# Hybrid encoder layer on one core: six pairs of projection units by seven half products, rotary rows turned in groups

## The chip, the cores and the metric

The kernel runs on one core of one Trainium2 chip. The metric is the device time of one execution in microseconds (us); what counts is the median of several runs, and a change is worth telling from about 0.2% on.

## What is computed

One encoder layer on 512 tokens of 1024 channels, in float32. Two token mixers work on the same input: a windowed grouped-query attention (A: 16 query heads, 4 key and value heads, 64 wide, window 128, a sink logit for each head) and a mixture of three dilated window attentions (B: 3 groups of 4 heads). The first 16 channels of each head of q and k are rotated by position. Both mixers' outputs go through projections, are weighted by sigmoid gates, projected, normalised, and followed by a SwiGLU layer:

```python
proj = h @ w_in[l]
qa, ka, va, qb, kb, vb = jnp.split(proj, SPLITS, axis=-1)
qa = rope_partial(qa.reshape(b, s, A_Q_HEADS, HEAD_DIM), pos)
...                                   # ka, qb, kb are rotated likewise
o_a = windowed_gqa_sink(qa, ka, va, a_sink[l]).astype(h.dtype)
o_b = dilated_mixture(qb, kb, vb).astype(h.dtype)
gates = jax.nn.sigmoid(h @ w_gate[l] + b_gate[l])
g_a, g_b = jnp.split(gates, N_BRANCH, axis=-1)
mixed = g_a * (o_a @ w_br_a[l]) + g_b * (o_b @ w_br_b[l])
h = layer_norm(DN_ALPHA * h + mixed @ w_out[l], ln1_g[l], ln1_b[l])
f = (jax.nn.silu(h @ w_ff_gate[l]) * (h @ w_ff_up[l])) @ w_ff_down[l]
h = layer_norm(DN_ALPHA * h + f, ln2_g[l], ln2_b[l])
```

`rope_partial` of a pair (t1, t2) of 8 channels each is (t1·cos − t2·sin, t1·sin + t2·cos).

## The kernel before

**Products.** Every float32 operand is split into a high part (rounded, written by ScalarE or VectorE) and a low part (value minus high part, a subtraction on VectorE), both in the format fp32r that TensorE takes. A product is three matmuls: high·high, high·low, low·high. The work on the projections goes in units: 128 output channels for all 512 tokens. `unit` loads a unit's weights in two halves of 256 KB (`half_unit`: one DMA, one `split`), and `feat_x` runs 8 × 3 matmuls of 512 columns over the token tiles `xh`, `xl` (`feat_k`, L496 to L498) into one PSUM bank.

**The stages.** First x and the first weights come in pieces, and k0, q0 and v0 are multiplied as they land. Then the attention stage: units of q, k, gates (g), values (VA, V0, V12) and the attentions themselves (A0 to A3, B0 to B3: four blocks of queries each). One block of `unit_a` is scores, mask and row maximum (VectorE, L798), exp (ScalarE), reciprocal and normalisation (VectorE, L805, L739), turning of the probabilities by TensorE (L749), their split (the low part on VectorE, L754) and the product with the values, "p·v" (L815, L816). About 330 us from the start the branch projections, the output projection and the feed-forward stage follow.

**Rotary.** `rotate` takes a unit's result in PSUM, multiplies it by a table of cosines (L517), exchanges the two groups of 8 channels by a shuffle (L519), multiplies by a table of sines (L521) and adds (L523): four VectorE operations of 128×512 for each q or k unit, though only 16 rows of each 64 turn (the tables hold 1 and 0 elsewhere).

**Seven half products.** The feed-forward stage computes its units in pairs by the Strassen-Winograd scheme: the 2×2 blocks are (unit, half of the input channels) for the weights and (half of the input channels, half of the tokens) for the tokens. Weight forms A11, A12, A22 and S1 to S4 (sums), token forms B11, B21, B22 and T1 to T4; each of seven products has 12 matmuls of 256 columns (`Quad`, L1422 to L1424). S1 and S3 come from a load and a second, accumulating load by GpSimd's queue (`load_sum`, L368); S2 and S4 from an addition on VectorE.

**What sets the order.** `Program` is a list scheduler that runs while the kernel is built. Each operation has engines it may run on, a cost, what it reads and writes, and a priority: its place in the work of TensorE plus an offset (weights −130, results −100, normalisation −150; lower goes first). With a model of the engines it writes out one fixed sequence for each engine; on the chip each engine goes through its sequence in order, and waits where an input isn't there. `ORDER` gives the succession of the units. Buffers come from pools with limits: `ws` (weights as loaded, 6), `whl` (their high and low parts, 12), `att`, `gen`, and PSUM banks (3 for `dense`).

Of the kernel before, what the change touches and what calls it, by code (L numbers as in the profile page):

```python
# [9 lines left out]
F32 = mybir.dt.float32  # L10
# [49 lines left out]
BANKS = dict(dense=3, s=2, tb=2, o=1, d=8)  # L60
UNITS = 2
SPIN = 4

# [4 lines left out]
X_PACE = {1: None}  # L68
N_WS, N_WHL, N_ATT = 6, 12, 16

# [47 lines left out]
class Program:  # L118
# [67 lines left out]
    def run(self):  # L186
# [26 lines left out]
        while n_left:  # L213
# [11 lines left out]
            while progress:  # L225
                progress = False
                for e in engines:
# [88 lines left out]
def hybrid_layer(ctx: ExitStack, tc: tile.TileContext, wpack, xT, xtok, sink, bgate,  # L316
# [8 lines left out]
    pr = Program({"slot": N_SLOT, "bank": 8, **BANKS,  # L325
                  "ws": N_WS, "whl": N_WHL, "att": N_ATT, "gen": N_SLOT - 2 - N_ATT - N_WS - N_WHL,
                  "unit": UNITS, "st": 4, "x4": 4, "wf": N_WF})
# [46 lines left out]
    def cp_alts(n, ps=False, cut=0.0):  # L374
        return [(ACT, act(n, ps) + cut), (DVE, dve(n, not ps) + cut)]
# [79 lines left out]
    got = {}  # L455
    for j in range(KD):
        st, ap = slot(F32, "xs"), FIRST["x"][j]

        for c0, c1 in ((0, S // 2), (S // 2, S)) if j == 0 else ((0, S),):
# [49 lines left out]

    EV, NORM = -100.0, -150.0  # L510


    SHUF = list(range(8, 16)) + list(range(0, 8)) + list(range(16, 32))

    def rotate(ps):
        R, Sh = slot(), slot()
        op([(DVE, dve(S))], lambda e: nc.vector.tensor_tensor(halves(R.t), back(ps.t), halves(cosT.t), op=ALU.mult),  # L517
           reads=[ps, cosT], writes=[R], prio=EV)
        op([(DVE, dve(S, extra=0.03))], lambda e: nc.vector.stream_shuffle(halves(Sh.t), back(ps.t), SHUF), reads=[ps], writes=[Sh],  # L519
           prio=EV)  # L520
# [131 lines left out]
    def turned_values(u, nt, turn_by=0, done=None):  # L652
# [3 lines left out]
        for i in range(2):  # L656
# [15 lines left out]

            op(cp_alts(S, True, 0.3 if turn_by else 0.1)[:2 if turn_by else 1], evac, reads=[ps], writes=[t], prio=EV)
            src.append(t)
# [325 lines left out]
    away = {}  # L1000

    def gate(f, put=False):
        ps = bank("dense")
# [34 lines left out]
    load(mB, maskb, prio=0)  # L1038
    env = {"gate": 0, "qs": {}, "ks": {}}

    def step(w):
        if w == "VA":
            env["va"] = turned_values(U_VA, 4, 0, psv)
# [14 lines left out]
        elif w[0] in "QK":  # L1058
            pair, g = int(w[1]), int(w[2])
            u = U_QKB + 6 * pair + 2 * g + (w[0] == "K")  # L1060
# [201 lines left out]

    def copy_by_act(dst, src, n, ps, reads, writes, prio=NORM):
        op([(ACT, act(n, ps))], lambda e: copy(ACT, dst(), src()), reads=reads, writes=writes, prio=prio)

    h1h4, h1l4 = [x4(), x4()], [x4(), x4()]
# [39 lines left out]

    LO, HI = slice(0, HP), slice(HP, S)
    su, uf = {}, {}
    silus = []

    def tt(dst, x, y, o, reads, writes, w=HP, prio=EV):
        op([(DVE, dve(w))], lambda e: nc.vector.tensor_tensor(dst(), x(), y(), op=o), reads=reads, writes=writes,  # L1312
           prio=prio)

    def parts(h, l, src, reads, n, prio, whole=True):

        copy_by_act(h[0], src, n, False, reads, [h[1], l[2]], prio)
        tt(l[0], src, lambda: f32(h[0]()), ALU.subtract, [*reads, h[1]], [l[1]], n, prio)

    def hl(st, prio):  # L1320
        h, l = slot(F32R, "whl"), slot(F32R, "whl")
        parts((lambda: h.t, h), (lambda: l.t, l, (l, "room")), lambda: st.t, [st], S, prio)
        return h, l

# [450 lines left out]
```

## Time and profile before

| | |
|---|---|
| median of 3 runs | 737.42 us (737.29 to 737.45) |
| the profiled execution | 737.0 us, span 735.2 us |
| granted TensorE clock | 0.999 |
| TensorE / VectorE / ScalarE busy | 99% / 89% / 61% of the span |
| matmuls | 4479, starting with the warm-up |
| DMA | 120.17 MB, 163 GB/s over the span |

A row of the profile names the line of the kernel, the engine, the operation and the tiles (out<-in by the program's names: `ps` is a PSUM bank, `sl` a slot in SBUF, `x` a part of the tokens). Helpers that record many operations have one line for all of them, as L357 (copy on ScalarE) and L1312 (VectorE operation on two tensors). The time that one matmul takes overlaps with the next; the price of a matmul in a stream is the distance between two starts.

### The profile page before, as it was taken

To read this page: it belongs to the slowest core of one execution; us is meant where nothing else is said; L and a number is where in the kernel's file an instruction comes from. 1 tells how busy PE (TensorE), PEld (TensorE's weight loads), DVE (VectorE), ACT (ScalarE), POOL (GpSimd) and SP (SyncE) were. 2 spreads that over 40 slices of the span, in tenths; PEclk is the share of its full clock that TensorE was granted. 3 is DMA by queue.
4 is the path that set the end of the run, shared out by engine and by line. 5 is a ranking of instruction groups with operands and counts; after the bars stand their busy time and mean duration, and the time that the engine had idled before them with its cause. 6 is when DMAs were issued, how large, how long until landed. Compare 5 with 4: busy or idle time off the path is not lost.

```text
span 735.2 us, 13431 instructions
## 1 busy us (share of the span) xinstructions
PE 725.2 (99%) x4479; PEld 663.0 (90%) x4479; DVE 653.7 (89%) x1428; ACT 447.4 (61%) x1012; POOL 109.5 (15%) x273
## 2 busy tenths in 40 slices
PE   9999999999999999999999999999999999999995
PEld 6888888888888889888888999999999999999985
DVE  5879998898898999897686999799999999899977
ACT  5647687757665657774352567656666556666721
POOL 0000110000003323500010002111102111202100
PEclk9999999999999999999999999999999999999999
DMA  8824523437234765455583389776888978978402
GB/s 270 289 58 144 163 82 87 129 94 204 76 93 138 201 176 163 137 170 174 165 205 88 86 250 233 178 179 154 203 254 195 221 196 237 243 196 180 112 29 86
DMA packets 69252, 120.17 MB, mean 163 GB/s; under 512 B 8576, under 2 KB 12800, under 8 KB 69184
## 3 DMA queue, kind: packets, MB, share of 16 engines
q1 hardware_dynamic: 59040, 101.10, 44.7%
q0 software_dynamic: 9872, 18.09, 15.2%
q8 instruction: 35, 0.57, 0.3%
q14 instruction: 33, 0.27, 0.1%
q10 hardware_dynamic: 272, 0.13, 0.1%
HBM read 103.04 MB, written 2.10 MB: 143 GB/s over the span
## 4 chain that ended last, share of the span: by engine, by line
PE 94%; DMA 2%; DVE 2%; SPq 1%; ACT 1%; issue 0%; DVEq 0%; ACTq 0%
PE ps L497 12%; PE ps L496 12%; PE ps L498 12%; PE ps L1422 9%; PE ps L1424 9%; PE ps L1423 9%; PE ps L1633 4%; PE ps L1635 4%; PE ps L1634 4%; PE ps L749 3%; PE ps L1192 3%; PE ps L1193 3%; PE ps L1194 3%; PE ps L647 1%; PE ps L646 1%; PE ps L815 1%
## 5 line engine op out<-in xcount | busy, mean ns | idle before, releaser
L357 ACT ACTIVATE sl<-sl 128x512 fp32r<-128x512 f32 (+3 forms) x383 | 210.6, 582 | 62.0 <-DVE sl L1312 17.3
L1312 DVE TENSOR_TENSOR sl<-sl,sl 128x512 fp32r<-128x512 f32 (+3 forms) x294 | 167.1, 609 | 6.2 <-ACT sl L357 3.4
L357 ACT ACTIVATE sl<-ps 128x256 f32<-128x256 f32 (+5 forms) x205 | 85.8, 441 | 99.7 <-PE ps L1424 60.1
L496 PE MATMUL ps<-x,sl 128*128 128x512 f32 (+1 forms) x369 | 142.4, 386 | 0.3 <-ACT x L357 0.3
L498 PE MATMUL ps<-x,sl 128*128 128x512 f32 (+1 forms) x369 | 139.8, 379 | 0.0
L497 PE MATMUL ps<-x,sl 128*128 128x512 f32 (+1 forms) x337 | 127.9, 379 | 0.2 <-DVE x L469 0.2
L1422 PE MATMUL ps<-sl,sl 128*128 128x256 f32 x352 | 96.9, 275 | 0.6 <-ACT sl L357 0.6
L1423 PE MATMUL ps<-sl,sl 128*128 128x256 f32 x352 | 96.8, 275 | 0.0
L1424 PE MATMUL ps<-sl,sl 128*128 128x256 f32 x352 | 96.8, 275 | 0.0
L383 DVE TENSOR_TENSOR sl<-sl,sl 128x512 fp32r<-128x512 f32 x130 | 87.2, 685 | 5.1 <-ACT sl L357 4.5
L498 PEld LDWEIGHTS ps<-x,sl 128*128 128x128 f32 x369 | 69.9, 189 | 9.9 <-DVE sl L406 0.2
L496 PEld LDWEIGHTS ps<-x,sl 128*128 128x128 f32 x369 | 70.2, 190 | 8.7 <-ACT x L357 0.5
L371 POOL DMA_DIRECT2D sl<-wpack x44 | 38.5, 883 | 260.3 <-DMA sl<-wpack 72.7
L1422 PE MATMUL ps<-x,sl 128*128 128x256 f32 x264 | 72.6, 275 | 0.0
L1423 PE MATMUL ps<-x,sl 128*128 128x256 f32 x264 | 72.6, 275 | 0.0
L1424 PE MATMUL ps<-x,sl 128*128 128x256 f32 x264 | 72.6, 275 | 0.0
L497 PEld LDWEIGHTS ps<-x,sl 128*128 128x128 f32 x337 | 64.0, 190 | 7.5 <-DVE x L469 0.5
L1422 PEld LDWEIGHTS ps<-sl,sl 128*128 128x128 f32 x352 | 67.6, 192 | 0.8 <-ACT sl L357 0.7
L1423 PEld LDWEIGHTS ps<-sl,sl 128*128 128x128 f32 x352 | 67.6, 192 | 0.1
L1424 PEld LDWEIGHTS ps<-sl,sl 128*128 128x128 f32 x352 | 67.6, 192 | 0.0
L1422 PEld LDWEIGHTS ps<-x,sl 128*128 128x128 f32 x264 | 50.6, 192 | 0.4
L1423 PEld LDWEIGHTS ps<-x,sl 128*128 128x128 f32 x264 | 50.6, 192 | 0.4
(151 smaller groups left out, 1547.1 us busy)
## 6 DMA issues: line engine op xcount, KB each, us to landing
sl<-wpack SPq DMA_DIRECT2D x243, 256.0 KB, 3.7
sl<-sl SPq DMA_DIRECT2D x108, 128.0 KB, 2.3
wf<-wpack SPq DMA_DIRECT2D x51, 256.0 KB, 5.0
sl<-wpack POOLq DMA_DIRECT2D x44, 256.0 KB, 5.9
wf<-wpack POOLq DMA_DIRECT2D x24, 256.0 KB, 6.3
sl<-xtok SPq DMA_DIRECT2D x8, 256.0 KB, 3.3
out<-sl SPq DMA_DIRECT2D x7, 256.0 KB, 2.0
sl<-xT SPq DMA_DIRECT2D x6, 256.0 KB, 5.6
```

The lines of the kernel that those rows point to most:

```text
L357: nc.scalar.activation(dst, src, AF.Copy)
L371: op([(POOL, 1.0)], lambda e: nc.gpsimd.dma_start(b.t, src2, accum_op=ALU.add), reads=[b], writes=[b], prio=prio, moves=1.65)
L383: op([(DVE, dve(S))], lambda e: nc.vector.tensor_tensor(l.t, src.t, f32(h.t), op=ALU.subtract), reads=[src, h], writes=[l], prio=prio, abs ...
L496: mm(o, a, x0, start=(k == 0 and begins), stop=False, skip_group_check=split)
L497: mm(o, a, x1, start=False, stop=False, skip_group_check=split)
L498: mm(o, b, x0, start=False, stop=(k == nk - 1), skip_group_check=split)
L1312: op([(DVE, dve(w))], lambda e: nc.vector.tensor_tensor(dst(), x(), y(), op=o), reads=reads, writes=writes, prio=prio)
L1422: mm(o, wh, pairs(bh[k]()), start=(first and k == 0), stop=False, skip_group_check=True)
L1423: mm(o, wh, pairs(bl[k]()), start=False, stop=False, skip_group_check=True)
L1424: mm(o, wl, pairs(bh[k]()), start=False, stop=(k == 3), skip_group_check=True)
L1633: mm(ps.t, x0, pairs(w[0].t), start=(first and m == 0), stop=False, skip_group_check=True)
L1634: mm(ps.t, x0, pairs(w[1].t), start=False, stop=False, skip_group_check=True)
```

## The change

1. **Pairs.** Six pairs of units (q2 and q3; k1 and q4; three of gates and gates or q5; q6 and q7) are computed by seven half products of 12 matmuls of 256 columns (`pair_x`). Seven weight forms are split for a pair instead of four half units; results are kept by copies of ScalarE and combined on VectorE.
2. **Token forms.** `x_forms` makes T1 to T4 from the loaded tiles of x, in place: 16 VectorE operations of half width and 8 splits, with priority −60.
3. **Rotary in groups.** q and k units now stand in SBUF: those of pairs come so, twelve unpaired ones by `in_sbuf`. At each R of `ORDER`, `turn_rows` gathers the 16 rows of each head of up to four tiles into one tile by DMAs of SP (two in and two back for a tile, 16×512 each), and turns them by four VectorE operations in all. 19 units go this way in six groups, three are rotated as before. The tables for it are put together by eight small DMAs, four of which double what is there.
4. **Gates.** Those of pairs come from SBUF; five of them are written to DRAM and fetched back in the branch stage.
5. **Order and model.** `ORDER` is written anew; `ws` and `whl` have 8 and 16 buffers up to the mark L, `gen` has 61 instead of 49, and the model's costs of SP, of GpSimd's DMAs and of their landing are higher up to 300 us.

```diff
-N_WS, N_WHL, N_ATT = 6, 12, 16
+N_WS, N_WHL, N_ATT, N_GEN = 6, 12, 16, 61
...
 ORDER = """
-g2 VA q1 A0 q2 q3 A1 g k1 q4 g q5 A2 g q6 g q7 A3 g2
-Q00 K00 Q01 K01 V12 Q02 K02 V0 B0 Q10 K10 B1 Q11 K11 Q12 K12 B2 B3 g8
+X g2 VA q1 A0 P:q2,q3 P:k1,q4 R A1 P:g,g P:q5,g P:q6,q7 R A2 P:g,g A3 g2 L Q00 K00 Q01 K01 R V12 Q02 K02 R V0 B0 Q10 K10 Q11 K11 R B1 Q12 K12 R B2 B3 g7
 """
+FORMS = -60.0
+PACK = -60.0
+BY_DMA = ()
+AWAY = range(8, 16)
+N_WSA, N_WHLA = 8, 16
...
-                        end = now + 0.47
-                        moved = max(moved, now + 0.9) + (1.5 if now < 5 else 0.92) * cost
-                        o.done = moved + 0.87
+                        end = now + (0.55 if now < SLOW else 0.47)
+                        moved = max(moved, now + 0.9) + (1.5 if now < 5 else 1.0 if now < SLOW else 0.92) * cost
+                        o.done = moved + (1.6 if 5 < now < SLOW else 0.87)
                     elif o.moves:
                         end = now + cost
-                        moved = max(moved, end + 0.3) + 0.92 * o.moves
-                        o.done = moved + (0.87 if e == ACT else 2.2)
+                        moved = max(moved, end + 0.3) + (1.0 if now < SLOW else 0.92) * o.moves
+                        o.done = moved + (0.87 if e == ACT else 3.2 if now < SLOW else 2.2)
...
+    def x_forms():
+        at = lambda k, n: (lambda b=xs[k]: b.t[:, n * HP:(n + 1) * HP])
+        key = lambda k: [(xs[k], 0), (xs[k], S // 2)] if k == 0 else [(xs[k], 0)]
+        for k in range(KD // 2):
+            a, b = key(k), key(k + 4)
+            x11, x12, x21, x22 = at(k, 0), at(k, 1), at(k + 4, 0), at(k + 4, 1)
+            def minus_sum(dst, x, y):
+                op([(DVE, dve(HP))], lambda e: nc.vector.scalar_tensor_tensor(
+                    dst(), x(), -1.0, y(), op0=ALU.mult, op1=ALU.subtract), reads=a + b, writes=b, prio=FORMS)
+            tt(x11, x11, x12, ALU.subtract, a, a, HP, FORMS)
+            tt(x12, x22, x12, ALU.subtract, a + b, a, HP, FORMS)
+            minus_sum(x22, x11, x22)
+            minus_sum(x21, x22, x21)
+            for kk, toks in ((k, a), (k + 4, b)):
+                h, l = slot(F32R), slot(F32R)
+                parts((lambda h=h: h.t, h), (lambda l=l: l.t, l, (l, "room")), lambda b=xs[kk]: b.t, toks, S, FORMS)
+                XP[kk] = (h, l)
...
+        def fetch(key):
+            st = W[key] = slot(F32, "ws")
+            if key[0] == "A":
+                load(st, part(key[1:]), prio=-LOOK)
+            else:
+                load_sum(st, part({"S1": "21", "S3": "11"}[key]), part({"S1": "22", "S3": "21"}[key]), -LOOK)
...
+        for key in ("A11", "S1", "A12", "S3", "A22"):
+            fetch(key)
+        sep("A11")
+        sep("A12")
+        form("S2", "A11", "S1", "A11")
+        sep("S2")
+        sep("S1")
+        form("S4", "A12", "A12", "S2")
+        for key in ("S3", "S4", "A22"):
+            sep(key)
+        y, xz, t, v = bank("dense"), bank("dense"), slot(), slot()
...
+        product("A11", "B11", y, "y", LO, True)
+        keep(t, LO, 1, y, "y", LO)
+        product("A12", "B21", xz, "x", LO, True)
+        product("S2", "T2", y, "y", LO, False)
+        keep(t, HI, 2, y, "y", LO)
+        product("S1", "T1", xz, "z", HI, True)
+        keep(v, HI, 2, xz, "z", HI)
+        product("S3", "T3", y, "y", LO, False)
+        product("S4", "B22", xz, "z", HI, False)
+        both = lambda: t.t.rearrange("p (c a b) -> p c a b", c=2, a=2)
+        tt(both, both, lambda: xz.t.rearrange("p (c b a) -> p c a b", c=2, a=2), ALU.add,
+           [(t, 1), (t, 2), (xz, "x"), (xz, "z")], [(t, 1), (t, 2)], S)
+        op([(DVE, dve(HP))], lambda e: nc.vector.scalar_tensor_tensor(
+            halves(v.t[:, HI]), back(y.t[:, LO]), -1.0, halves(v.t[:, HI]), op0=ALU.mult, op1=ALU.subtract),
+           reads=[(v, 2), (y, "y")], writes=[(v, 2)], prio=EV)
+        product("A22", "T4", y, "y", LO, False)
+        keep(v, LO, 1, y, "y", LO, -1.0)
+        env["mark"] = pr.ops[-1]
+        return t, v
...
+    def turn_rows(tiles):
+        c, s_ = packed()
+        G, H = slot(), slot()
+        n = 32 * len(tiles)
+        gs = []
+        for i, R in enumerate(tiles):
+            for h in range(2):
+                gs.append((G, 2 * i + h))
+                op([(SP, 0.1)], lambda e, R=R, i=i, h=h: nc.sync.dma_start(
+                    G.t[32 * i + 16 * h:32 * i + 16 * h + 16], R.t[64 * h:64 * h + 16]), reads=[(R, 1), (R, 2)], writes=[gs[-1]], prio=EV)
+        g, h_ = (lambda: G.t[0:n]), (lambda: H.t[0:n])
+        op([(DVE, dve(S, extra=0.03))], lambda e: nc.vector.stream_shuffle(h_(), g(), SHUF2), reads=gs, writes=[H], prio=EV)
+        op([(DVE, dve(S))], lambda e: nc.vector.tensor_tensor(g(), g(), c.t[0:n], op=ALU.mult),
+           reads=[*gs, *[(c, i) for i in range(4)]], writes=gs, prio=EV)
+        op([(DVE, dve(S))], lambda e: nc.vector.tensor_tensor(h_(), h_(), s_.t[0:n], op=ALU.mult),
+           reads=[H, *[(s_, i) for i in range(4)]], writes=[H], prio=EV)
+        op([(DVE, dve(S))], lambda e: nc.vector.tensor_tensor(g(), g(), h_(), op=ALU.add), reads=[*gs, H], writes=gs, prio=EV)
+        for i, R in enumerate(tiles):
+            for h in range(2):
+                op([(SP, 0.1)], lambda e, R=R, i=i, h=h: nc.sync.dma_start(
+                    R.t[64 * h:64 * h + 16], G.t[32 * i + 16 * h:32 * i + 16 * h + 16]),
+                   reads=gs, writes=[(R, "r", h)], prio=EV)
+            op([(POOL, 0.0)], lambda e: None, reads=[(R, "r", 0), (R, "r", 1)], writes=[R], prio=EV)
+    def in_sbuf(u):
+        ps, t = bank("dense"), slot()
+        feat_x(ps, unit(u))
+        op([(ACT, act(S, True))], lambda e: copy(ACT, halves(t.t), back(ps.t)), reads=[ps], writes=[(t, 1), (t, 2)], prio=EV)
+        return t
...
+    def gate_of(f, t):
+        gz[f] = t
+        op([(ACT, act(S, False, 1))], lambda e: nc.scalar.activation(
+            t.t, t.t, AF.Tanh, bias=bg.t[:, f:f + 1], scale=0.5), reads=[(t, 1), (t, 2), bg], writes=[t], prio=EV)
+        if f in AWAY:
+            put_away(f)
+    def put_away(f):
+        t, d = gz[f], Buf("dram", None, lambda: dram.tile([P, S], F32, name=name("gz")))
+        op([(SP, 0.73)], lambda e: nc.sync.dma_start(d.t, t.t), reads=[t], writes=[d], prio=EV)
+        away[f] = d
...
+        if w == "X":
+            x_forms()
+        elif w == "L":
+            op([(POOL, 0.0)], lambda e: pr.limits.update(ws=N_WS, whl=N_WHL), after=[env["mark"]])
+        elif w[:2] == "P:":
+            both = [units_of(x) for x in w[2:].split(",")]
+            for (u, f), t in zip(both, pair_x(*[u for u, _ in both])):
+                if u < U_GATE:
+                    env["turn"].append((t, f))
+                else:
+                    f(t)
+        elif w[:2] == "T:":
+            u, f = units_of(w[2:])
+            env["turn"].append((in_sbuf(u), f))
+        elif w == "R":
+            tiles = [t for t, _ in env["turn"]]
+            turn_rows(tiles)
+            done_rows.update(tiles)
+            for t, f in env["turn"]:
+                f(t)
+            env["turn"] = []
...
-            if w[0] == "Q":
-                env["qs"][pair, g] = dense_q(u, 4 if g == 0 else 0, (0, 1))
-            else:
-                env["ks"][pair, g] = dense_k(u, 8 if g == 0 else 0)
+            u, f = units_of(w)
+            env["turn"].append((in_sbuf(u), f))
```

How the instructions stand, at three places. First VectorE's sequence ahead of the second p·v of A0's first block, before (L754 writes the low parts that the p·v takes; L383 is a split of weights; L517 to L523 are `rotate`; L739 the normalisation):

```order
L798 ISA st_597 128x1
L521 TENSOR_TENSOR sl_700<-sl_700,sl_190 128x512
L739 TENSOR_SCALAR sl_541<-sl_541,st_560 128x256
L523 TENSOR_TENSOR sl_691<-sl_691,sl_700 128x512
L383 TENSOR_TENSOR sl_716<-sl_516,sl_715 128x512
L805 RECIPROCAL st_597<-st_597 128x4
L739 TENSOR_SCALAR sl_578<-sl_578,st_597 128x384
L580 TENSOR_TENSOR sl_735<-sl_691,sl_734 128x512
L754 TENSOR_TENSOR sl_746<-ps_729,sl_745 128x512
L754 TENSOR_TENSOR sl_756<-ps_738,sl_755 128x512
```

And now (L968 is what L754 was, L953 what L739 was; L534 is the helper's line for splits and sums of pairs and token forms, L652 a combination of a pair's products, L365 the copy of the turned probabilities):

```order
L534 TENSOR_TENSOR sl_903<-sl_726,sl_902 128x512
L652 SCALAR_TENSOR_TENSOR sl_907<-ps_713,sl_907 128x256
L1019 RECIPROCAL st_753<-st_753 128x4
L534 TENSOR_TENSOR sl_926<-sl_648,sl_925 128x512
L953 TENSOR_SCALAR sl_676<-sl_676,st_753 128x384
L365 CAST sl_964<-ps_934 128x512
L534 TENSOR_TENSOR sl_940<-sl_736,sl_939 128x512
L968 TENSOR_TENSOR sl_965<-ps_934,sl_964 128x512
L534 TENSOR_TENSOR sl_756<-sl_756,ps_819 128x512
L968 TENSOR_TENSOR sl_968<-ps_943,sl_967 128x512
```

Before, rotary work and single weight splits stand between the last normalisation and the low part `sl_756`; now there are the splits of the first pair and the next, and combinations of the first pair's products. The low part `sl_968` is VectorE's 136th row; `sl_756` was its 103rd (tiles are numbered anew in each program: `sl_756` of now is a result of the first pair).

Second, TensorE's sequence at the same place, before (L496 to L498 are a unit's matmuls, L815 and L816 the p·v):

```order
L496 MATMUL ps_760<-x_94,sl_566 128x512
L497 MATMUL ps_760<-x_103,sl_566 128x512
L498 MATMUL ps_760<-x_94,sl_567 128x512
L815 MATMUL ps_776<-sl_745,sl_486 128x512
L816 MATMUL ps_776<-sl_746,sl_486 128x512
L815 MATMUL ps_776<-sl_755,sl_488 128x512
L816 MATMUL ps_776<-sl_756,sl_488 128x512
```

And now (L629 to L631 are a pair's matmuls, L1029 and L1030 the p·v, L963 the turning of the next block's probabilities):

```order
L629 MATMUL ps_713<-sl_575,sl_777 128x256
L630 MATMUL ps_713<-sl_576,sl_777 128x256
L631 MATMUL ps_713<-sl_575,sl_778 128x256
L1029 MATMUL ps_995<-sl_964,sl_551 128x512
L1030 MATMUL ps_995<-sl_965,sl_551 128x512
L963 MATMUL ps_1002<-ident,sl_673 128x128
L963 MATMUL ps_1002<-ident,sl_676 128x128
L963 MATMUL ps_1002<-ident,sl_678 128x128
L963 MATMUL ps_1002<-ident,sl_680 128x128
L1029 MATMUL ps_995<-sl_967,sl_553 128x512
L1030 MATMUL ps_995<-sl_968,sl_553 128x512
```

What stands directly ahead of the p·v was a unit by 512 columns and is a pair's half product by 256; the second p·v, with `sl_756`, was TensorE's row 305 and is, with `sl_968`, its row 411.

Third, VectorE's start now (L486 the low parts of x, L422 those of the first weights, in pieces):

```order
L534 TENSOR_TENSOR sl_73<-sl_73 128x256
L422 TENSOR_TENSOR sl_108<-sl_83,sl_107 128x128
L486 TENSOR_TENSOR x_101<-sl_71,x_93 128x512
L422 TENSOR_TENSOR sl_117<-sl_87,sl_116 128x128
L534 TENSOR_TENSOR sl_71<-sl_71 128x256
L486 TENSOR_TENSOR x_101<-sl_103,x_93 128x512
L534 TENSOR_TENSOR sl_103<-sl_103 128x256
L422 TENSOR_TENSOR sl_99<-sl_75,sl_98 128x256
L422 TENSOR_TENSOR sl_108<-sl_83,sl_107 128x256
L422 TENSOR_TENSOR sl_117<-sl_87,sl_116 128x256
L486 TENSOR_TENSOR x_101<-sl_144,x_93 128x512
L534 TENSOR_TENSOR sl_144<-sl_144 128x256
```

The rows L534 here are token forms; they stand among the splits of the first weights and of x, where there was nothing between those.

More of the change, by code (lines that the diff above doesn't have):

```diff
@@ L61 @@
 UNITS = 2
+SLOW = 300
 SPIN = 4
@@ L390, in half_unit, with low_by_dma @@
         load(st, wpack[u, :, j * S:(j + 1) * S], prio=-LOOK)
+        if j == 1 and u in BY_DMA:
+            low_by_dma(st, h, l, wpack[u, :, j * S:(j + 1) * S], -LOOK)
+            return h, l
         split(st, h, l, prio=-LOOK, hold=[(l, "room")])
         return h, l
+    def low_by_dma(st, h, l, src, prio):
+        op(cp_alts(S), lambda e: copy(e, h.t, st.t), reads=[st], writes=[h, (l, "room")], prio=prio)
+        op([(ACT, act(S))], lambda e: nc.scalar.activation(l.t, st.t, AF.Copy, scale=-1.0), reads=[st], writes=[l], prio=prio)
+        op([(POOL, 1.0)], lambda e: nc.gpsimd.dma_start(l.t, src.bitcast(F32R), accum_op=ALU.add), reads=[l],
+           writes=[l], prio=prio, moves=1.65)
     pieces = {}
@@ new lines, in hybrid_layer, with packed @@
+    packs = []
+    SHUF2 = [x + y for x in (0, 16) for y in SHUF[:16]]
+    def packed():
+        if not packs:
+            packs.extend((slot(), slot()))
+            for b, src in zip(packs, (ropec, ropes)):
+                for i in range(2):
+                    op([(SP, 0.1)], lambda e, b=b, src=src, i=i: nc.sync.dma_start(b.t[16 * i:16 * i + 16], src[0:16]),
+                       writes=[(b, i)], prio=PACK)
+                for n in (32, 64):
+                    op([(SP, 0.1)], lambda e, b=b, n=n: nc.sync.dma_start(b.t[n:2 * n], b.t[0:n]),
+                       reads=[(b, i) for i in range(4) if i < n // 16 and i < 3], writes=[(b, n // 32 + 1)], prio=PACK)
+        return packs
@@ L515, in rotate @@
+    def in_sbuf(u):
[3 more added lines that the diff above has]
+        return t
     def rotate(ps):
+        if ps in done_rows:
+            return ps
+        if "slot" in ps.keys:
+            return turned(ps)
         R, Sh = slot(), slot()
```

105 lines of the change are left out of this document (86 added, 19 removed).

## The prediction

> **What bounds the kernel now.** I read the page first (span, busy shares, chain), then the waits of TensorE, then a table of stretches. "PE" is TensorE's matmuls, "PEld" its weight loads, "DVE" VectorE, "ACT" ScalarE; numbers are us.
>
> ```profile
> span 735.2 us, 13431 instructions
> ...
> PE 725.2 (99%) x4479; PEld 663.0 (90%) x4479; DVE 653.7 (89%) x1428; ACT 447.4 (61%) x1012; POOL 109.5 (15%) x273
> ...
> PE 94%; DMA 2%; DVE 2%; SPq 1%; ACT 1%; issue 0%; DVEq 0%; ACTq 0%
> ```
>
> TensorE is busy 99% of the span and is 94% of the chain that ended last. All waits of its queue for other engines (total, number of waits, longest):
>
> ```profile
> PE ps L433 <- DVE eps L483: 1.2, 1, 1.2
> PE ps L1422 <- ACT sl L357: 0.6, 1, 0.6
> PE ps L1192 <- DVE sl L1126: 0.4, 1, 0.4
> PE ps L496 <- ACT x L357: 0.3, 1, 0.3
> PE ps L497 <- DVE x L469: 0.2, 1, 0.2
> ```
>
> That is 2.7 us in all, and the first and largest lies at the program's start. So removed waits can give next to nothing; removed TensorE time counts in full, as long as nobody else becomes late. VectorE, at 89%, is the one that could. The stretches (length, then PE, PEld, DVE, ACT, POOL busy with instruction counts, granted clock, DMA share, GB/s):
>
> ```profile
> 0.00:64.30 64.30, 62.61 (x294) 52.63 (x294) 49.48 (x109) 38.19 (x82) 5.10 (x21) 1.00 0.61 197
> 0.00:22.00 22.00, 20.31 (x84) 15.32 (x85) 12.99 (x30) 12.78 (x25) 2.44 (x13) 1.00 0.83 272
> 22.00:36.60 14.60, 14.60 (x69) 12.79 (x68) 14.21 (x26) 10.31 (x19) 0.12 (x1) 1.00 0.83 293
> 40.68:64.30 23.62, 23.62 (x123) 20.93 (x122) 22.27 (x55) 14.03 (x36) 2.54 (x8) 1.00 0.38 101
> 60.00:120.00 60.00, 60.00 (x325) 53.70 (x324) 54.71 (x141) 45.96 (x106) 5.05 (x17) 1.00 0.45 128
> 440.00:460.00 20.00, 20.00 (x182) 20.00 (x181) 19.93 (x42) 14.67 (x34) 5.91 (x7) 1.00 0.99 239
> ```
>
> VectorE already works 14.21 of 14.60 us at 22 to 36.6. Its idle time up to 64.30, which matters below, is 64.30 − 49.48 = 14.8 us, 22.00 − 12.99 = 9.0 of it in the first 22 us.
>
> **The products: what is removed.** Starts of consecutive matmuls in the timeline (start, duration), of a 512-column unit and of a 256-column one in the feed-forward stage, which works by seven half products already:
>
> ```profile
> 45.06 0.38 PE L496 MATMUL ps<-x,sl 128*128 128x512 f32 x1
> ...
> 47.43 0.38 PE L498 MATMUL ps<-x,sl 128*128 128x512 f32 x1
> ...
> 420.00 0.28 PE L1422 MATMUL ps<-x,sl 128*128 128x256 f32 x1
> ...
> 421.56 0.28 PE L1424 MATMUL ps<-x,sl 128*128 128x256 f32 x1
> ```
>
> The first two rows are 11 matmuls apart: 2.37/11 = 0.2155 each. The last two are 14 apart: 1.56/14 = 0.1114. The durations overlap, so the pitch is the price. Two units cost 48 × 0.2155 = 10.34; as a pair, 7 products × 12 matmuls × 0.1114 = 9.36. Six pairs save 6 × 0.98 = **5.9 us of TensorE time**. No other matmul is removed or added; turned rows and kept tiles go through no matmul.
>
> [...] The row for the weight loads of the half-width matmuls (busy, mean ns):
>
> ```profile
> L1422 PEld LDWEIGHTS ps<-sl,sl 128*128 128x128 f32 x352 | 67.6, 192 | 0.8 <-ACT sl L357 0.7
> ```
>
> One takes 192 ns while matmuls start every 111 ns, with PEld 20.00 of 20 us busy at 440 to 460 and PE still without a wait: the loads overlap each other. [...]
>
> **VectorE's added work and the place where it is due.** Starts in its timeline give its prices:
>
> ```profile
> 441.36 0.42 DVE L1312 TENSOR_TENSOR sl<-sl 128x256 f32<-128x256 f32 x1
> 441.70 0.41 DVE L1312 TENSOR_TENSOR sl<-sl,ps 128x256 f32<-128x256 f32 x1
> ...
> 442.70 0.68 DVE L1312 TENSOR_TENSOR sl<-sl,sl 128x512 fp32r<-128x512 f32 x1
> 443.30 0.42 DVE L1446 SCALAR_TENSOR_TENSOR sl<-sl,sl 128x256 f32<-128x256 f32 x1
> ...
> 22.61 0.73 DVE L519 STREAM_SHUFFLE sl<-ps 128x512 f32<-128x512 f32 x1
> 23.24 2.04 DVE L383 TENSOR_TENSOR sl<-sl,sl 128x512 fp32r<-128x512 f32 x3
> ```
>
> A half-width operation costs 0.34, a full one 0.60, a shuffle 0.63. Over the whole stage the change about balances: 62 more splits and sums, 16 token forms and 12 half-width combinations more, against 24 fewer splits elsewhere and about 50 rotary operations saved by turning up to four tiles at once; I count +8 to +10 us in some 300. But it adds at the front: token forms and the first pairs' splits come before the rotary savings. The tight place is the second p·v of A0's first block. Its rows before, and those for VectorE's first work and longest wait (idle time before in brackets):
>
> ```profile
> 3.78 0.42 DVE L469 TENSOR_TENSOR x<-sl,x 128x256 fp32r<-128x256 f32 x1 [2.64 <-ACT x L357]
> ...
> 40.68 0.76 DVE L695 TENSOR_TENSOR sl<-ps,sl 128x256 fp32r<-128x256 f32 x2 [4.07 <-ACT sl L357]
> ...
> 62.32 1.29 DVE L754 TENSOR_TENSOR sl<-ps,sl 128x512 fp32r<-128x512 f32 x2
> ...
> 64.30 0.38 PE L815 MATMUL ps<-sl,sl 128*128 128x512 f32 x1
> ```
>
> VectorE finishes the low part at 62.32 + 1.29 = 63.6; TensorE takes it one matmul after 64.30, at 64.5.
> - TensorE ahead of that matmul: 253 → 175 matmuls of 512, 16 → 196 of 256, and four more of 128: −78 × 0.2155 + 180 × 0.1114 + 4 × 0.11 = +3.7. The pairs' work has been drawn ahead, so TensorE could be there at 64.5 + 3.7 = 68.2.
> - VectorE ahead of it: 53 → 71 full operations, 10 → 28 half ones, two shuffles fewer, three casts of x fewer against two normalisations more (about −0.5): 18 × 0.60 + 18 × 0.34 − 1.3 − 0.5 = +15.1. At the old idle time it would be done at 63.6 + 15.1 = 78.7, 10.5 late.
> - Of the 14.8 idle, 3.8 lie before the first data and stay. The 4.07 before 40.68 go, since VectorE is then behind. Of the other 5.2 in the first 22 us, 12 of the 24 token-form operations stand among the first splits and fill perhaps half, 2.6. Of the 1.7 behind 22 us I give it 0.4. Sum 7.1: the stall is 10.5 − 7.1 = 3.4, say **3.5 us**. Bounds: all 11.0 recovered, no stall (below zero it cannot go: no PE wait is removed here); only the 4.07 recovered, 6.4; none, 10.5.
>
> Behind this place TensorE's work grows faster than VectorE's by the same prices: VectorE's lead improves by 0.5 at the p·v 12.5 us of TensorE work later, by 1.2 at 37.7, by 2.9 at 61, and by over 5 from 70 on. So no second stall at full pace; but at the 5.7% idle of 40.68 to 64.30 (1.35 of 23.62) 37.7 us lose 2.1 against 1.2, another 1.0 (the most of these places).
>
> **The rest.** ScalarE gets 24 keep copies, 12 copies of unpaired units, eight token and 18 more weight copies: by these rows about 32 us over the stage, and perhaps 10 by the tight place, on top of 38.19 of 64.30: cover enough, no price. DMA:
>
> ```profile
> L357 ACT ACTIVATE sl<-sl 128x512 fp32r<-128x512 f32 (+3 forms) x383 | 210.6, 582 | 62.0 <-DVE sl L1312 17.3
> L357 ACT ACTIVATE sl<-ps 128x256 f32<-128x256 f32 (+5 forms) x205 | 85.8, 441 | 99.7 <-PE ps L1424 60.1
> ...
> sl<-wpack SPq DMA_DIRECT2D x243, 256.0 KB, 3.7
> sl<-sl SPq DMA_DIRECT2D x108, 128.0 KB, 2.3
> ...
> sl<-wpack POOLq DMA_DIRECT2D x44, 256.0 KB, 5.9
> ```
>
> A sum of weights now needs a load (3.7) and an accumulating one behind it (5.9): 9.6 until S1 can be used, by VectorE for S2, with everything behind it in VectorE's order waiting. Loads are queued with eight buffers, 1.6 pairs ahead (five buffers each), some 15 us; that hides 9.6 unless the DMAs are full, as at 0.83 of 22 to 36.6. I price it at nothing, at most 3 us once. The 76 moves of 16 rows (32 KB) stand in no row; the nearest is 2.3 for 128 KB. In and back is 4.6 to 7 with the turn, and SP holds weight loads behind the moves back until VectorE has turned the group; those scores come tens of us after the tiles are finished, so: nothing, at most 2 us. [...] Gates put away and fetched, table doubling: hidden the same way.
>
> **Sum.** 737.0 (profiled execution; span 735.2 and 1.8 around it) − 5.9 + 3.5 = 734.6. The median is 0.4 higher than that execution, so 735.0. In general: 737.4 − 5.9 + stall = 731.5 + stall.
>
> **The rivals.** 0.2%, 1.5 us, is about what a measurement of this kernel can tell; the same lies from 735.9 to 738.9, that is a stall of 4.4 to 7.4.
> 1. Forecast, stall 1.5 to 4.4: 733.0 to 735.9. Chance 0.43.
> 2. All hidden: VectorE recovers nearly all 11.0 us. 731.5 to 733. For it: 19.93 of 20 us at 440 to 460, where it is saturated. Against: the early gaps are waits for data. 0.11.
> 3. The gain eaten by waits: only the 4.07 recovered (6.4: 737.9), or the forecast plus 1.0, or plus 3 for a late S1 (736.0, 738.0). 735.9 to 738.9. 0.19.
> 4. Slower: VectorE's idle time consists of dependent waits (ScalarE's high part, then the subtraction; score, row maximum, exp) that stay when it is behind. Then the stall is 10.5 at the tight place, and at the 8.8% idle of 60 to 120 (5.29 of 60) the next 61 us lose 5.4 against 2.9, 2.5 more: up to 13.0, so 738.9 to 744.5. It decides from a stall of 7.4 on. For it: in every early stretch VectorE is short of full though never waited for. Against: 97% at 22 to 36.6. 0.25.
> 5. The weight loads bound the half products: 84 × 0.192 = 16.1 a pair against 10.34, +5.8 each, 772. Against it stand the 111 ns. [...]
>
> The range holds cases 1 to 3 (0.73) and the lower part of case 4, to 741: 731.5 to 741.0. Faster: cases 1 and 2, 0.54; same: 0.19; slower: 0.27.
>
> **What would show it.** Right: matmul time per pair about 9.4 at a pitch of 0.111; TensorE waits of 2 to 4 us, all on VectorE, between 45 and 75 us and mostly ahead of a p·v (L1030); VectorE above 95% busy from 10 to 70 us; hardly a wait later. Wrong: waits of TensorE or VectorE on DMA (sums, 16-row moves), stalls spread over 75 to 200 us, or a busy share of VectorE there that stays near 91%.

## The result and the profile after

| | before | changed |
|---|---|---|
| median, us | 737.38 (737.29 to 737.45, 4 runs) | 749.27 (747.13 to 752.02, 4 runs) |
| ratio | | 1.0163, 95% interval 1.0130 to 1.0197 |
| span of the profiled execution, us | 735.2 | 747.3 |
| granted TensorE clock | 0.999 | 0.993 |

The change makes the kernel slower by 11.9 us, where 735.0 was forecast with a range up to 741.0. By the prediction's own formula, 731.5 + stall, the stall is 17.8 us and not 3.5. From the page of the changed kernel, the rows that answer to those shown of before:

```profile
span 747.3 us, 14121 instructions
...
PE 726.0 (97%) x4695; PEld 667.3 (89%) x4695; DVE 659.4 (88%) x1436; ACT 470.4 (63%) x1067; POOL 123.8 (17%) x285
...
PE 78%; DMA 8%; DVE 7%; SPq 3%; issue 2%; ACT 2%; DVEq 0%; ACTq 0%
```

The chain that ended last was 94% TensorE; now DMA, VectorE and SP's queue have 18% of it, and VectorE is not busier over the span than it was. TensorE's own waits, the longer ones (total, number, longest):

```profile
PE ps L513 <- DVE sl L1387: 3.5, 1, 3.5
PE ps L895 <- ACT sl L363: 2.2, 1, 2.2
PE ps L1029 <- ACT sl L363: 1.3, 1, 1.3
...
PE ps L629 <- ACT sl L637: 1.2, 1, 1.2
PE ps L1195 <- DVE sl L968: 1.1, 1, 1.1
PE ps L1030 <- DVE sl L968: 0.9, 2, 0.5
```

No wait names SP. To find what stands behind them, each stall has to be followed back through the engine that TensorE waited for. First a map. If the start of each matmul is set against the pitch of its width (0.2155 for 512 columns, 0.162 for 384, 0.1114 for 256, 0.109 for 192 and 128), what is over is lost time. Worked out so from the starts in the traces, in us, for this kernel and for four of the experiments below ("whole run" has the end of the feed-forward stage too):

| stretch | before | changed | moves_half | dve_light | no_away | no_away_half |
|---|---|---|---|---|---|---|
| 0 to 20 | 3.7 | 3.5 | 3.2 | 4.3 | 4.2 | 3.7 |
| 20 to 70 | 0.1 | 3.7 | 3.1 | 0.8 | 4.5 | 2.8 |
| 70 to 140 | 0.1 | 4.2 | 0.6 | 4.1 | 3.0 | 0.5 |
| 140 to 220 | 0.2 | 4.1 | 0.2 | 2.0 | 0.2 | 0.2 |
| 220 to 330 | 0.5 | 1.8 | 0.5 | 4.2 | 3.4 | 1.2 |
| 330 to 420 | 0.9 | 5.9 | 5.9 | 5.6 | 0.5 | 0.5 |
| whole run | 6.9 | 24.6 | 15.0 | 22.5 | 17.2 | 10.2 |

So 17.7 us are lost beyond before, in three kinds of places. **At 40**, the turning of the values (timeline of TensorE, ScalarE and VectorE; idle time before, and what ended it, in brackets):

```profile
42.16 0.55 PE L895 MATMUL ps<-ident,sl 128*128 128x128 f32 x3 [2.18 <-ACT sl L363]
...
40.42 1.15 ACT L363 ACTIVATE sl<-sl 128x512 fp32r<-128x512 f32 x2 [2.17 <-DVE sl L534]
41.47 0.64 ACT L363 ACTIVATE sl<-ps 128x256 f32<-128x256 f32 x2
...
36.89 4.04 DVE L534 TENSOR_TENSOR sl<-sl,sl 128x512 f32<-128x512 f32 x7
```

TensorE waits for ScalarE's copies out of PSUM (41.47); ScalarE holds them behind high parts (40.42) whose inputs VectorE still had to form, in an unbroken row of seven splits and sums. This is VectorE's pace.

**At 200**, SP's queue, then ScalarE and VectorE, then TensorE:

```profile
181.68 10.11 SPq L801 DMA_DIRECT2D sl<-sl  x16
191.88 5.03 SPq L846 DMA_DIRECT2D sl<-sl  x8
197.01 3.87 SPq L371 DMA_DIRECT2D sl<-wpack  x8
...
200.63 1.27 ACT L363 ACTIVATE sl<-sl 128x512 fp32r<-128x512 f32 x2 [2.52 <-DMA sl<-wpack]
...
201.29 1.34 DVE L389 TENSOR_TENSOR sl<-sl,sl 128x512 fp32r<-128x512 f32 x2 [2.87 <-ACT sl L363]
...
202.44 0.48 PE L1029 MATMUL ps<-sl,sl 128*128 128x512 f32 x1 [1.31 <-ACT sl L363]
203.28 0.48 PE L1030 MATMUL ps<-sl,sl 128*128 128x512 f32 x1 [0.36 <-DVE sl L968]
```

When a group of four tiles has been turned, the moves that bring their high and low parts into place (L801, L846) all become ready at once: 24 of them, 0.63 us each on SP's queue, 15 us. Eight weight loads stand behind and are issued at 197.01 only. ScalarE's copy of the first of these weights waits 2.5 us, VectorE's split waits for ScalarE, and the p·v, whose parts come later in both engines' sequences, waits for them. In before, the longest such row has a third of the moves and of the time:

```profile
78.71 4.95 SPq L587 DMA_DIRECT2D sl<-sl  x8
```

The waits at 105 to 120 and 298 in the changed kernel follow like rows, of 15 moves from 92.04 and of 24 from 275.54. Two of those at 105 to 120 come by another way through the same queue: at 108 ScalarE's keep copy waits for the write of a gate, and at 115 VectorE's turn of a group waits for the 16-row moves that bring its rows; a p·v waits behind it.

```profile
108.38 0.38 ACT L637 ACTIVATE sl<-ps 128x256 f32<-128x256 f32 x1 [0.87 <-DMA gz<-sl]
...
115.56 0.01 DVE L705 LOAD_MASK_SELECT sl<-sl  x1 [1.69 <-DMA sl<-sl]
```

**At 384**, in the branch stage:

```profile
388.40 0.71 PE L513 MATMUL ps<-sl,sl 128*128 128x512 f32 x1 [3.55 <-DVE sl L1387]
388.90 0.63 PE L514 MATMUL ps<-sl,sl 128*128 128x512 f32 x1
...
385.11 0.69 DVE L534 TENSOR_TENSOR sl<-sl,sl 128x512 f32<-128x512 f32 x1 [2.96 <-DMA sl<-wpack]
387.06 0.69 DVE L534 TENSOR_TENSOR sl<-sl,sl 128x512 f32<-128x512 f32 x1 [1.26 <-DMA sl<-wpack]
387.67 0.68 DVE L1387 SCALAR_TENSOR_TENSOR sl<-sl,ps 128x512 f32<-128x512 f32 x1
...
376.84 2.77 POOL L377 DMA_DIRECT2D sl<-wpack  x3 [43.37 <-DMA sl<-wpack]
...
380.00:385.00 5.00, 4.86 (x23) 3.92 (x21) 2.16 (x4) 1.04 (x2) 0.00 (x0) 1.00 1.05 290
```

VectorE waits for weight sums of the feed-forward stage whose accumulating loads GpSimd issued from 376.84 on; they land 8 us later, with the DMAs full (last row: share 1.05) of fetched gates, normalisation vectors and x. The gate product L1387, which frees the PSUM bank for TensorE, stands behind in VectorE's order. After this wait TensorE starts a matmul every 0.43 us (388.90 to 391.89) instead of 0.216: another 1.7 us. Late landing alone is not new here: in before, the accumulating loads issued from 365 to 385 land after 7.9 us in the median, with a DMA share of 1.08 at 370 to 375, and TensorE loses 0.9 us in the whole stretch from 330 to 420.

### The profile page after: what moved, and what is told of

Read it like the earlier page. It is cut to its first block, busy times and chain, and to the rows that moved or that the text cites. A ratio compares the mean times of both kernels' runs of the same rounds, so it can differ in the third digit from the quotient of the medians.

```text
span 747.3 us, 14121 instructions
## 1 busy us (share of the span) xinstructions
PE 726.0 (97%) x4695; PEld 667.3 (89%) x4695; DVE 659.4 (88%) x1436; ACT 470.4 (63%) x1067; POOL 123.8 (17%) x285
## 3 DMA queue, kind: packets, MB, share of 16 engines
HBM read 109.20 MB, written 3.41 MB: 151 GB/s over the span
## 4 chain that ended last, share of the span: by engine, by line
PE 78%; DMA 8%; DVE 7%; SPq 3%; issue 2%; ACT 2%; DVEq 0%; ACTq 0%
PE ps L1665 9%; PE ps L1663 9%; PE ps L1664 9%; PE ps L513 7%; PE ps L514 7%; PE ps L515 7%; PE ps L1874 4%; PE ps L1876 4%; PE ps L1875 4%; DMA sl<-wpack 4%; DVE sl L534 3%; PE ps L1453 3%; PE ps L1454 3%; PE ps L1455 3%; DMA sl<-sl 2%; PE ps L963 2%
## 5 line engine op out<-in xcount | busy, mean ns | idle before, releaser
L363 ACT ACTIVATE sl<-sl 128x512 fp32r<-128x512 f32 (+2 forms) x412 | 226.8, 584 | 60.6 <-DVE sl L534 19.4
L534 DVE TENSOR_TENSOR sl<-sl,sl 128x512 fp32r<-128x512 f32 (+3 forms) x360 | 209.9, 622 | 10.0 <-DMA sl<-wpack 4.2
L363 ACT ACTIVATE sl<-ps 128x256 f32<-128x256 f32 (+6 forms) x214 | 90.3, 442 | 94.8 <-PE ps L1665 60.1
L513 PE MATMUL ps<-x,sl 128*128 128x512 f32 (+1 forms) x273 | 106.2, 389 | 0.0
L515 PE MATMUL ps<-x,sl 128*128 128x512 f32 (+1 forms) x273 | 104.1, 381 | 0.0
L377 POOL DMA_DIRECT2D sl<-wpack x56 | 49.0, 886 | 323.6 <-DMA sl<-wpack 153.8
L514 PE MATMUL ps<-x,sl 128*128 128x512 f32 (+1 forms) x241 | 92.3, 383 | 0.3 <-DVE x L486 0.2
L389 DVE TENSOR_TENSOR sl<-sl,sl 128x512 fp32r<-128x512 f32 x106 | 71.1, 686 | 10.4 <-ACT sl L363 8.8
L515 PEld LDWEIGHTS ps<-x,sl 128*128 128x128 f32 x273 | 52.2, 191 | 7.4
L513 PEld LDWEIGHTS ps<-x,sl 128*128 128x128 f32 x273 | 52.2, 191 | 6.3 <-ACT x L363 0.4
L514 PEld LDWEIGHTS ps<-x,sl 128*128 128x128 f32 x241 | 46.1, 191 | 6.2 <-DVE x L486 1.2
L1663 PEld LDWEIGHTS ps<-x,sl 128*128 128x128 f32 x264 | 50.6, 192 | 0.4
L1664 PEld LDWEIGHTS ps<-x,sl 128*128 128x128 f32 x264 | 50.6, 192 | 0.4
```

The lines of the kernel that those rows point to most:

```text
L363: nc.scalar.activation(dst, src, AF.Copy)
L377: op([(POOL, 1.0)], lambda e: nc.gpsimd.dma_start(b.t, src2, accum_op=ALU.add), reads=[b], writes=[b], prio=prio, moves=1.65)
L389: op([(DVE, dve(S))], lambda e: nc.vector.tensor_tensor(l.t, src.t, f32(h.t), op=ALU.subtract), reads=[src, h], writes=[l], prio=prio, abs ...
L513: mm(o, a, x0, start=(k == 0 and begins), stop=False, skip_group_check=split)
L514: mm(o, a, x1, start=False, stop=False, skip_group_check=split)
L515: mm(o, b, x0, start=False, stop=(k == nk - 1), skip_group_check=split)
```

## The experiments

Three theories: **Q**, rows of moves on SP's queue hold weight loads; **V**, VectorE's pace; **D**, gates put away and fetched. Ratios are to before on the same chip.

**moves_half**, Q against V, in the changed kernel's order:

```diff
-        op([(SP, 0.4)], lambda e: nc.sync.dma_start(f32(dst.t[d:d + 64]), f32(src.t[c:c + 64])), reads=[src],
+        op([(SP, 0.4)], lambda e: None if key == 'h' else nc.sync.dma_start(f32(dst.t), f32(src.t)), reads=[src],
```

(and the same for L846).

> The changed kernel in the same order, but the moves of finished q and k tiles (L801, L846) are merged two by two into one DMA of the whole tile: half as many issues on SP's queue, the same bytes (the high or low half of a tile is wrong by it). Theory Q (a group turned together releases up to 24 moves at once, SP issues one every 0.63 us, and the weight loads queued behind them come some 15 us late): the stalls at 105 to 120, 200 to 207 and 298 shrink or go, 740 to 745 us against 749.3. Theory V (VectorE is behind because of token forms and splits): nothing of VectorE's changes, 748 to 750.

740.27 us (10 runs), ratio 1.0038 (1.0026 to 1.0050): 9.0 less. SP's queue at the same place, and all of TensorE's waits but the first at the start:

```profile
177.39 5.09 SPq L801 DMA_DIRECT2D sl<-sl  x8
182.65 2.43 SPq L846 DMA_DIRECT2D sl<-sl  x4
185.19 5.21 SPq L371 DMA_DIRECT2D sl<-wpack  x8
...
PE ps L513 <- DVE sl L1387: 3.3, 1, 3.3
PE ps L895 <- ACT sl L363: 2.4, 1, 2.4
...
PE ps L1663 <- ACT sl L363: 0.5, 1, 0.5
PE ps L629 <- DVE sl L652: 0.2, 1, 0.2
```

The row takes 7.5 us instead of 15.1, and every stall between 70 and 330 is gone, with the bytes the same and VectorE's work untouched. Q holds for them. A move that is not issued holds no slot either, so the edit takes away half of the issues and the hold on half of the slots that the moves read; these two were not separated.

**dve_light**, V, in the same order: `b.t[:, n * HP:(n + 1) * HP]` becomes `b.t[:, n * HP:n * HP + 8]` in `x_forms`, and likewise in the sums and combinations.

> The changed kernel in the same order, but 46 VectorE operations that the pairs brought (16 token forms, 12 weight sums S2 and S4, 18 combinations) work on 8 columns only: some 17 us of VectorE's time gone, every wait kept (what they compute is wrong). Theory V: the stall at 39.7 (2.3) and those that end on VectorE at 56, 116 and 120 (1.7) go, and if VectorE's pace stands behind the others too, up to 10: 739 to 745. Theory Q: at most the 2.3 at 39.7, 746.5 to 748.

745.95 us, ratio 1.0105 (1.0088 to 1.0122): 3.3 less, a little below the range of Q and above that of V. The gain lies between 20 and 70 (3.7 to 0.8); 70 to 140 stays at 4.1, and of the later stretches 140 to 220 loses less (4.1 to 2.0) and 220 to 330 more (1.8 to 4.2). V holds for the stall at 40; the waits at 105 to 120 stay.

**rows_only**: `T:q2 T:q3 ...` instead of `P:q2,q3`, no X.

> Rotary in groups alone: all units by 48 matmuls as before, no token forms, no pairs; q2, q3, k1, q4, q5, q6, q7 and the twelve Q and K units kept by ScalarE and turned in the same six groups. TensorE's work is that of before, VectorE has some 50 operations less (30 us). Theory Q: the bursts stay, 741 to 746. Theory V: 736 to 738, as before.

740.52 us, ratio 1.0038 (1.0025 to 1.0052), a little below the range of Q and outside V's. The one place behind the start that loses (most of 4.8 us, at 289 to 296) follows a row of 24 moves:

```profile
268.88 10.37 SPq L801 DMA_DIRECT2D sl<-sl  x16
279.34 6.08 SPq L846 DMA_DIRECT2D sl<-sl  x8
...
286.79 3.37 SPq L371 DMA_DIRECT2D sl<-wpack  x7
```

So the groups cost time without any pair, although they take some 50 operations from VectorE (x1375 instead of x1428). Rows as long at 86.7 (20 moves) and 194.0 (24) do no harm here: two units take four loads for 10.3 us of TensorE, where a pair takes five of SP and two of GpSimd for 9.4, so loads behind a row should be due sooner beside pairs; this was not tried by itself.

**pairs_only**: no R, each tile by `rotate`, 53 `gen` buffers.

> Pairs alone: six pairs by seven half products, but each q and k unit turned by its own four VectorE operations as before, no row moves (and 53 instead of 61 general buffers). TensorE saves 5.9, VectorE has some 46 full operations (28 us) more than the changed kernel. Theory Q: no groups, no bursts, so 733 to 742 with what is left of the stalls at 40 and 384. Theory V: VectorE falls far behind, 752 or more.

767.34 us, ratio 1.0403 (1.0387 to 1.0418). V, and far over: VectorE is busy 95 of the 100 us from 40 to 140, and nearly 23 us are lost between 20 and 140; some 8 of them are the clock, at 0.92 in these 100 us (last but two in the row). So these pairs, in this order, can't be had without the groups: both theories are true, each where the other's remedy is taken away.

```profile
40.00:140.00 100.00, 87.46 (x630) 81.60 (x629) 95.09 (x218) 65.94 (x155) 11.32 (x27) 0.92 0.63 160
```

**no_away**: `AWAY = ()`.

> The changed kernel without gates put away: all gates stay in SBUF, nothing is written to DRAM and fetched back. Theory D (at 375 to 385 the fetched gates crowd the DMAs together with the normalisation vectors and three accumulating loads, VectorE waits for a late weight sum and TensorE behind it 3.7 us, then runs 1.9 us at half clock): the stall at 384 goes, 743 to 746. Rival D2 (the sum is late because the loads ahead of it find their buffers late, VectorE being full at 340 to 370): 748 to 751.

741.08 us, ratio 1.0043 (1.0029 to 1.0057): 8.2 less, more than D said. The stall at 384 is gone (5.9 to 0.5 in 330 to 420). The order changes with it: 140 to 220 loses nothing any more and 220 to 330 loses 1.6 more. That putting gates away brings the stall at 384 is shown; whether by its transfers or by the order that goes with it was not separated, and the DMAs are no emptier without them (share 0.87 at 365 to 385 here, 0.83 in the changed kernel).

The stall at 200 went too, though the row of moves that stood before it is still there:

```profile
181.53 10.68 SPq L801 DMA_DIRECT2D sl<-sl  x16
192.38 4.95 SPq L846 DMA_DIRECT2D sl<-sl  x8
197.38 6.55 SPq L371 DMA_DIRECT2D sl<-wpack  x9
```

So a row of 24 is not enough for a stall, as rows_only showed at 86.7 and 194.0: what stands behind it must also be due.

**no_away_half**, both (half of each moved tile is left out, as in moves_half):

> Both at once: no gate put away, and the moves of finished q and k tiles merged two by two as in moves_half (half of each tile is wrong by it). Theories Q and D add: of the changed kernel's time above 731.5 only the stall at 40 (2.5, theory V) and small ones are left, 733 to 736. If one stall only hid the other, 738 or more.

734.57 us, ratio 0.9964 (0.9953 to 0.9976), 0.4% faster than before. Of the stalls that the change brought only the one at 40 is left (2.8 in 20 to 70). The last matmul starts 2.6 us earlier than before with 3.3 more lost: the pairs save 5.9. The two remedies overlap: alone they gave 9.0 and 8.2, together 14.7.

The other six look for a kernel that computes everything and keeps this. None does: nothing here that computes the whole layer is faster than before. **half_pool** gives 38 of the 110 moves to GpSimd, half of those of L801 and none of L846 (`[(POOL, 0.95) if by_pool else (SP, 0.4)]`):

> The changed kernel computing the same, with half of the moves of finished q and k tiles (the low parts and second copies) issued by GpSimd's queue instead of SP's, known to the scheduler. Theory Q: SP's bursts are half as long, the stalls at 105, 200 and 298 go, 739 to 743. Rival: GpSimd's own issues, 0.87 us each, come late in turn and scores wait for them, 747 or more.

749.38 us, ratio 1.0161 (1.0145 to 1.0176): no gain. The time is in the rival's range. The loss at 200 goes (4.1 to 0.2), but 8.8 are lost in the branch stage; the whole order shifts, so the rival's cause is not shown either.

**small_groups**: R after each pair, and after Q10 K10.

> The changed kernel with groups of two tiles instead of four (three more groups): bursts of 8 to 12 moves. Theory Q: 741 to 745. Theory V: VectorE has 12 operations more, 7 us, 750 or more.

745.95 us, ratio 1.0115 (1.0091 to 1.0139), above the range of Q and below that of V: 3.3 less, with 6.3 lost at 70 to 140.

**forms20**: `FORMS = -20.0`.

> The changed kernel with the token forms 40 us of TensorE work less ahead in priority (-20 instead of -60). Theory V for the first stall only (VectorE is full with token forms and weight splits at 20 to 40, ScalarE's queue waits for it and the turning of values behind): the 2.3 at 39.7 goes, 746 to 748. Rival: the forms come too late for the first pair's products, which wait instead, 749 or more.

750.50 us, ratio 1.0171 (1.0156 to 1.0186). The time is in the rival's range, and not clearly different from the changed kernel. The stall at 40 is 1.8 instead of 2.3, and the stalls at 107, 200, 298 and 384 are still there: moving VectorE's work a little didn't help where it is full.

**fix_act**: no gates away, and in `q_post`

```diff
-            move(t, a, x, a, "h", [(t, "room")])
+            op(cp_alts(S), lambda e, t=t, a=a: copy(e, t.t[a:a + 64], f32(x.t[a:a + 64])), reads=[x],
+               writes=[(t, "h"), (t, "room")], prio=EV)
```

> A kernel that computes the same as the reference: no gate put away, and the high halves of finished q tiles written in place by copies of ScalarE or VectorE (64x512 each) instead of SP's moves, known to the scheduler; k tiles as before. Theories Q and D: 734 to 738. Rival: ScalarE's in-order queue, with some 30 copies of 0.6 us more, becomes late and p·v waits for it, 741 or more.

740.66 us, ratio 1.0045 (1.0032 to 1.0059), no better than no_away. TensorE now loses time to ScalarE's keep copies (1.5 us at 89.7, 1.0 at 53.6): copies that replace moves (64x512) stand ahead of them.

**fix_pool**: `nc.gpsimd.tensor_tensor` for eight of the forms.

> As fix_act, and 8 of the 16 token forms on GpSimd, which does little up to 28 us. Theory V for the stall at 40: 1 to 2 us less than fix_act. Rival: GpSimd is slower at them than the 0.6 us it is priced at, and the first pair waits for its tokens, 1 to 3 us more than fix_act.

743.62 us, ratio 1.0084 (1.0070 to 1.0098), 3.0 more than fix_act, as its rival said, but for another reason. GpSimd's forms and VectorE's operations slow each other (both engines' timelines; L422 is a split of weights, L564 a token form):

```profile
12.81 0.69 DVE L422 TENSOR_TENSOR sl<-sl,sl 128x512 fp32r<-128x512 f32 x1
15.44 1.21 DVE L422 TENSOR_TENSOR sl<-sl,sl 128x512 fp32r<-128x512 f32 x1
...
6.16 0.73 POOL L564 TENSOR_TENSOR sl<-sl 128x256 f32<-128x256 f32 x1 [4.17 <-DVE x L486]
12.93 1.17 POOL L564 TENSOR_TENSOR sl<-sl,sl 128x256 f32<-128x256 f32 x1 [2.55 <-DMA sl<-xT]
14.05 1.18 POOL L564 TENSOR_TENSOR sl<-sl 128x256 f32<-128x256 f32 x1
```

The split takes VectorE 0.69 us where it starts ahead of GpSimd's form (12.81 and 12.93) and 1.21 where a form is under way (15.44); a form takes GpSimd 0.73 at 6.16 and 1.17 or 1.18 beside VectorE. TensorE waits 0.73 and 1.08 us for such splits, ahead of its starts at 16.70 and 18.70.

**fix_prio**: no gates away, `prio=-40.0` for the moves.

> A kernel that computes the same as the reference: no gate put away, and the moves of finished q and k tiles have priority -40 instead of -100, so that the scheduler puts weight loads that are ready between them (M a move, - a load: in the largest burst, MMMMMMM.. with five loads behind it becomes MM-MMM2M-MM2M2-MMMMM2M2M-M). No instruction more or less than no_away. Theory Q: loads are no longer held by a burst, the stalls at 290 and most of those at 107 go, 735.5 to 739 against 741.1 of no_away. Rival: the moves themselves come late for the scores, 741 or more.

743.89 us, ratio 1.0075 (1.0054 to 1.0096), against Q's number; that is 2.8 more than no_away, though the two intervals just touch, and two stretches at half pace (see the end) stand in this profile: matmuls of 512 columns start 0.43 apart from 43.82 on, those of 256 columns 0.21 apart from 111.91 on, and the granted clock is 0.994 (0.995 in no_away's). Its longest stall (2.9) is the second part of a p·v at 107.5, behind this on ScalarE:

```profile
107.42 0.38 ACT L637 ACTIVATE sl<-ps 128x256 f32<-128x256 f32 x1 [2.71 <-DMA sl<-sl]
```

A keep copy reads PSUM and writes a slot, so what it waits for must be the slot, which a move still uses. With loads ahead of moves, then, the moves are late instead. This narrows Q: another order of the same issues didn't help, half of the issues (and of the held slots) did.

## Why the prediction was wrong

- **Saving of TensorE: right.** 5.9 was said, and no_away_half gives 5.9 by a map that takes the pitches for granted; that they hold in the pairs is shown by the pairs' own matmuls, which start 0.111 apart (ten starts between the rows below). With that rival 5, 0.192 apart, fell; it had the 0.02 by which the 0.27 for slower exceeds rival 4's 0.25.

```profile
57.28 0.28 PE L630 MATMUL ps<-sl,sl 128*128 128x256 f32 x1
...
58.39 0.28 PE L631 MATMUL ps<-sl,sl 128*128 128x256 f32 x1
```

- **VectorE up to A0's p·v: right in size, wrong in place.** The p·v's last matmul starts at 71.7; 68.2 + 3.5 was said. But the loss lies ahead: 2.3 at the turning of values, where ScalarE's queue passes VectorE's lateness on, 0.4 at a pair's combination, 0.7 at scores that wait for a move. That the sum agrees is luck in part, since the 0.7 are SP's and none of the loss is at the p·v. VectorE's pace itself was seen rightly: it is busy 57.48 of the 60 us from 10 to 70, over 95% as said, and 23.90 of the 24 from 36 to 60, and dve_light removes most of the loss.

```profile
36.00:60.00 24.00, 21.62 (x158) 20.18 (x158) 23.90 (x53) 16.75 (x40) 6.41 (x11) 1.00 0.76 179
71.69 0.38 PE L1030 MATMUL ps<-sl,sl 128*128 128x512 f32 x1
```

- **The step that failed: "The rest", SP's queue.** I saw that SP holds weight loads behind moves, priced that for the 76 row moves alone (nothing, at most 2 us) and counted them as the only new thing on SP. What the groups do to the other moves was left out: 4 to 8 of each tile, once spread over the units, become ready together behind the turn. Its price stood in the trace of before, 4.95 us for 8 issues; 24 × 0.62 = 15 us against loads that I had 15 us ahead and needing 4 to 10 to land. Measured: halving these moves gives 9.0 us back (moves_half), of which 1.7 are a stretch at half clock that goes with the stall at 200; where the loads behind a row weren't due, it cost nothing (no_away at 200).
- **"Gates put away and fetched: hidden the same way"** failed too: 5 us at 384, 8.2 in the median without them. The cover I named, loads far ahead, isn't there: three accumulating loads, issued together at 376.84, land 8 us and more later, and VectorE waits. Whether the gates' own transfers make them late or the order that came with them stays open.
- **Rival 3** named a late S1 held by VectorE's order, the mechanism of 384, at 3 us once; it came in a stage that I had not looked at. **Rival 4** named the right side by another mechanism: VectorE's idle time at 60 to 120 (6.3 of 60 us) is waits, but 4.5 of it for SP's moves and loads themselves and little for ScalarE. The time lies beyond rival 4, which ended at 744.5, and short of rival 5's 772.
- **The signs of being wrong** were well chosen: stalls spread over 75 to 200 us came, and a wait of VectorE for 16-row moves (at 115.56, above).
- **The 16-row moves** themselves: 32 KB land in 2.5 us, 128 KB in 2.4, a quarter of the bytes for the same time; what cost most here was the issue, beside the one wait of 1.7 us at 115.

```profile
sl<-sl SPq DMA_DIRECT2D x110, 128.0 KB, 2.4
...
sl<-sl SPq DMA_DIRECT2D x76, 32.0 KB, 2.5
```

## What to carry to other kernels

Work that is gathered into groups is also released in groups: count what becomes ready at the moment a group ends, on every in-order queue, times the issue price of that queue (0.63 us a move on SP's here), and set it against how far ahead the transfers behind it stand. A stall that names ScalarE or VectorE is followed back through their own waits, here to a load two queues away. And a saving on the busiest engine is worth what the others leave of it: the 6 us were there throughout, and show only when moves and gate transfers no longer make it wait.

## What the hardware showed

A stall can cost more than its own length. After the 3.6 us at 384 TensorE starts matmuls 0.43 apart; after 1.3 and 0.4 us of waiting at 200 to 203 it does so as well, and the granted clock (the last but two of the window rows) is half in just these two stretches up to the last matmul, 3.41 us each, so 1.7 us lost each:

```profile
204.30 0.63 PE L514 MATMUL ps<-x,sl 128*128 128x512 f32 x1
204.72 0.63 PE L515 MATMUL ps<-x,sl 128*128 128x512 f32 x1
...
204.21:207.62 3.41, 3.41 (x9) 0.50 0.32 122
388.53:391.94 3.41, 3.41 (x9) 0.50 0.46 76
```

After the 2.2 us at 40 it doesn't: the starts from 42.77 to 44.27 are 0.21 or 0.22 apart. In fix_prio, after 2.2 us at the same place, it does:

```profile
42.67 0.55 PE L895 MATMUL ps<-ident,sl 128*128 128x128 f32 x3 [2.21 <-ACT sl L363]
...
43.82 0.63 PE L513 MATMUL ps<-x,sl 128*128 128x512 f32 x1
44.24 0.63 PE L514 MATMUL ps<-x,sl 128*128 128x512 f32 x1
```

What decides between the two was not shown. So a stall of 2 us cost 1.7 more or nothing here, and a part of the difference between two executions can be this: the four of the changed kernel go from 747.13 us at a granted clock of 0.995 to 752.02 at 0.991, and 0.004 of 750 us are 3 of the 4.9 between them, an estimate from these numbers.
